# The RWKV of the context between the products of three feed-forwards, in a two-block network on one core

## The chip, the core and the metric

One core of a Trainium2 chip runs the whole network in one launch. The metric is the device time of that launch in microseconds. The kernel before takes 2272.97 us (median of 3 runs, 2269.67 to 2284.12). The engines are PE (TensorE: matmuls; its weight loads are listed apart as PEld), DVE (VectorE), ACT (ScalarE), POOL (GpSimd) and SP (SyncE, which issues the DMAs). Each runs its own instructions in order.

## The reference

256 latent tokens of 1024 features pass through a first block and then, with 256 context tokens, through a second block. All is float32.

```python
def first_block(x, ...):
    for l in range(2):
        x = x + 0.5 * swiglu_ffn(rmsnorm(x, norm_ffn1[l]), ffn1_w_up[l], ffn1_w_down[l])
        x = x + hybrid_mixer(rmsnorm(x, norm_mix[l]), ...)      # pooling and an LRU
        x = x + 0.5 * swiglu_ffn(rmsnorm(x, norm_ffn2[l]), ffn2_w_up[l], ffn2_w_down[l])
    return rmsnorm(x, final_norm)

def second_block(x, c, ctx, c_ctx, ada_w, ada_b, norm_g, ...):
    xc = ctx
    for i in range(2):
        shift, scale, gate = split(silu(c) @ ada_w[i] + ada_b[i], 3)            # and the like of c_ctx
        h  = rms_norm(x,  norm_g[i]) * (1 + scale)   + shift
        hc = rms_norm(xc, norm_g[i]) * (1 + scale_c) + shift_c
        y, yc = rwkv7_mixer(h, hc, ...) if i == 0 else diff_mixer(h, hc, ...)   # attention
        x = x + gate * y;  xc = xc + gate_c * yc

def rwkv7_mixer(h, hc, ...):
    lat, con = rwkv7_streams(h, ...), rwkv7_streams(hc, ...)
    oc_f, sc_f = scan_direction(con, 0, zeros, False);  oc_b, sc_b = scan_direction(con, 1, zeros, True)
    ol_f, _    = scan_direction(lat, 0, sc_f, False);   ol_b, _    = scan_direction(lat, 1, sc_b, True)
    return readout(ol_f + ol_b, lat, ...), readout(oc_f + oc_b, con, ...)
```

The context's RWKV depends on `ctx` and on the modulation alone, and not on the first block. The latents' scans start from the states in which the context's scans end.

## The kernel before, in words

**Large products.** Every large product is made of float32r parts: an operand is split in a high and a low part, and three matmuls (high by high, high by low, low by high) make one step of 128 rows. A class `Weights` streams the weight chunks in the order of use through a ring: a DMA on SP's queue into a raw tile, then per 128x512 piece an ACT copy (`whi`) and a DVE subtraction (`wlo`; `vhi` and `vlo` in the second block). In the mixers a part of these pieces goes to POOL instead (`MIXLO`: numbers such as 4 mean that every fourth low, or high, piece does).

**The order of work** is written out by the program at build time. `Clock` keeps a rough account of the engines' times. Large products are emitted in a fixed order; between them `tick` and `advance` take steps of `Chain`s, which are generators of dependent instructions. A step is emitted once the account says that its inputs are there. A chain that is not `urgent` also waits until DVE and ACT are at most `BACKLOG` (600 ns) ahead of PE. `take` and `until` let the account's time go on (PE then stands idle) until a tile is free or a condition holds.

**Stages.** (1) The first block, latents alone: for each of two layers a feed-forward `f1`, the mixer, a feed-forward `f2`. A feed-forward has 44 upward column tiles (24 matmuls each) and 8 downward ones (66 each): 1584 matmuls of 128x256. A mixer has 1560. (2) `ada` (L1094) computes the modulation meanwhile: of each of 48 column tiles of `ada_w`, in two halves, POOL multiplies 128x512 weights with the two broadcast conditions, 128x1024 elements an instruction, and ACT sums the rows. It goes on only while `calm` is set, which is so in feed-forwards. (3) `enter_ctx` and `enter` (L1253, L1267) form the operands of RWKV; the first four products (`EARLY`) are done with the context's half while the last norm of the latents is computed. (4) `rwkv` (L1354): both sequences lie side by side in tiles of 512 tokens. For each of 8 tiles of 128 channels (j, called a head here) there are four products of 8 steps (k, r, v, gate), the lora products, and then chains: `prepare` (decays, keys, alpha and beta, one set of 9 work tiles `w`), `products` for each sequence (u = 0, 1: pairs of steps within a chunk, into `GE`), `inverse` (for both sequences at once: 32 problems by DVE transposes, 15 steps of two instructions on POOL, and small matmuls), `recur` for each direction (4 chunks of the context, then 4 of the latents, one after the other; each chunk has three groups of small matmuls with DVE or ACT between them), and `readout`. (5) `rwkv_out` (the output product of both sequences, with the first keys and values of the attention) and `attention`.

Most instructions are recorded with the one line L89, that of the helper that counts them, so groups are told apart by the names of their tiles: `ops` and `b` are operands of large products, `q` alpha and beta, `S` the state, `uv`, `rs`, `ro` tiles of the recurrence, `invX`, `invN`, `invt` those of the inverse, `X` also a part of `GE`.

Of the kernel before, what the change touches and what calls it, by code (L numbers as in the profile page):

```python
# [26 lines left out]
class Clock:  # L27
    """A rough account of when the engines get through what was emitted, to order the emission by."""
# [21 lines left out]
    def pressing(self):  # L50
        """Whether this tick can still get full, but only with nothing but large products in it."""
# [11 lines left out]
    def product(self, least, columns, rows):  # L63
        """A product; the array's clock is full in a tick after one with enough columns in it."""
# [8 lines left out]
class Engine:  # L73
    """An engine whose instructions are put on the clock's account."""
# [26 lines left out]
    def product(self, name, out, weights, moving):  # L101
# [3 lines left out]
        elif moving.dtype == F32R:  # L105
            self.clock.product(107, n + 5, rows)
        elif out.shape[0] > 64:
# [20 lines left out]
class Core:  # L128
    """The core's engines, with an account of their time."""
# [9 lines left out]
class Part(tuple):  # L139
    """The two parts of an operand, and when they are there."""  # L140
# [9 lines left out]
class Weights:  # L150
    """Streams weight chunks in the order of use and splits each into two float32r parts."""
# [26 lines left out]
    def queue(self, need=0):  # L178
        while self.queued < min(max(need, 0), len(self.plan)) or (
# [16 lines left out]
            hi = self.pool.tile([128, self.chunk], F32R, tag=self.tag + "hi", bufs=self.nsplit, name=self.tag + "hi")  # L196
            lo = self.pool.tile([128, self.chunk], F32R, tag=self.tag + "lo", bufs=self.nsplit, name=self.tag + "lo")
# [29 lines left out]
    def begin(self):  # L227
        """Splits what has been asked for, before anything else follows."""
# [17 lines left out]
    def tick(self, n):  # L246
        """Goes on with the splitting as far as the engines have time for it."""
# [10 lines left out]
    def get(self, key, keep=0):  # L258
        """The parts of the next chunk; the last `keep` chunks before it are still in use."""
# [18 lines left out]
class Lazy:  # L278
    """Operand pairs that exist once their chains have got there."""
# [12 lines left out]
class Joined:  # L292
    """Chunks that follow one another along the contraction, as one."""
# [8 lines left out]
class Row:  # L302
    """Sums of squares over the features, and what follows from them, for n tokens."""
# [7 lines left out]
AT_ONCE = "at once"  # L311


class Chain:
    """Dependent steps, and when the next of them can start; a step that yields AT_ONCE leaves
    the next one as ready as it was itself."""

    def __init__(self, gen, ready, urgent, rank):
        self.gen, self.ready, self.urgent, self.rank, self.end = gen, ready, urgent, rank, 0.0

# [4 lines left out]
class Base:  # L325
# [15 lines left out]
    def chain(self, gen, urgent=True, start=0.0, rank=0):  # L341
        """Takes up a chain, whose first step waits for `start`; those of a lower rank go first."""
        c = Chain(gen, max(self.clock.end, self.clock.t["PE"], start), urgent, rank)
        if start > self.clock.t["PE"]:
            self.enlist(c)
        else:
            self.step(c)
# [5 lines left out]
    def step(self, c):  # L353
# [11 lines left out]
        if go != AT_ONCE and moved:  # L365
            c.ready = c.end
# [25 lines left out]
    def between(self):  # L392
        """The chains get their turn between two products."""
# [15 lines left out]
    def arrive(self, t):  # L409
        """Lets the time until t go to the chains."""  # L410
# [1933 lines left out]
```

## Time and profile before

| | us |
|---|---|
| median of 3 runs | 2272.97 |
| lowest, highest | 2269.67, 2284.12 |
| span of the profiled execution | 2274.9 |
| PE, PEld busy | 2106.3, 1882.8 |
| DVE, ACT, POOL busy | 1717.8, 1287.4, 861.8 |

The span is that of one profiled execution. Busy time is the time in which an engine has an instruction in it; matmuls are pipelined, so PE counts as busy also where it could take more. The granted clock is the share of TensorE's 2.4 GHz, at 1.0 or 0.5 in any moment. Shares over the whole span hide that the stages have different limits, so the rows below are taken by stage. Stage limits are found by counting large matmuls in program order.

### The profile page before, as it was taken

To read this page: it belongs to the slowest core of one execution; us is meant where nothing else is said; L and a number is where in the kernel's file an instruction comes from. 1 tells how busy PE (TensorE), PEld (TensorE's weight loads), DVE (VectorE), ACT (ScalarE), POOL (GpSimd) and SP (SyncE) were. 2 spreads that over 40 slices of the span, in tenths; PEclk is the share of its full clock that TensorE was granted. 3 is DMA by queue.
4 is the path that set the end of the run, shared out by engine and by line. 5 is a ranking of instruction groups with operands and counts; after the bars stand their busy time and mean duration, and the time that the engine had idled before them with its cause. 6 is when DMAs were issued, how large, how long until landed. Compare 5 with 4: busy or idle time off the path is not lost. (4 is left out here: it accounts for less than half of the span.)

```text
span 2274.9 us, 47231 instructions
## 1 busy us (share of the span) xinstructions
PE 2106.3 (93%) x18172; PEld 1882.8 (83%) x18172; DVE 1717.8 (76%) x3076; ACT 1287.4 (57%) x2970; POOL 861.8 (38%) x1063
## 2 busy tenths in 40 slices
PE   8998998998889889989999988999999998999998
PEld 7988988998889889989999967677677667777878
DVE  6689898888878888897666675765766764558896
ACT  6666684666666666765556543354454342347565
POOL 1154565344544453562001153443543542312331
PEclk9999999999999999999999996899889877869999
DMA  7666554666666565456566310101100110215542
GB/s 243 207 190 202 159 167 131 213 204 200 195 211 209 189 199 193 149 156 197 187 187 183 121 57 24 34 25 39 38 28 30 32 40 9 59 52 165 148 121 89
DMA packets 114098, 300.41 MB, mean 132 GB/s; under 512 B 12624, under 2 KB 18512, under 8 KB 113744
## 3 DMA queue, kind: packets, MB, share of 16 engines
q1 hardware_dynamic: 113872, 297.39, 41.5%
q8 instruction: 142, 2.33, 0.4%
q14 instruction: 84, 0.69, 0.1%
HBM read 292.89 MB, written 4.46 MB: 131 GB/s over the span
## 5 line engine op out<-in xcount | busy, mean ns | idle before, releaser
L89 PE MATMUL ps<-ops,whi 128*128 128x256 f32 x4852 | 895.7, 282 | 19.9 <-ACT ops L89 9.2
L89 DVE TENSOR_TENSOR wlo<-wraw,whi 128x512 fp32r<-128x512 f32 (+2 forms) x792 | 675.4, 890 | 152.0 <-ACT whi L89 147.1
L89 PEld LDWEIGHTS ps<-ops,whi 128*128 128x128 f32 x4852 | 759.2, 190 | 23.9 <-ACT ops L89 9.4
L89 PE MATMUL ps<-ops,wlo 128*128 128x256 f32 x2504 | 710.2, 284 | 28.0 <-DVE wlo L89 28.0
L89 ACT ACTIVATE whi<-wraw 128x512 fp32r<-128x512 f32 (+2 forms) x798 | 437.4, 597 | 130.2 <-issue 60.2
L89 PEld LDWEIGHTS ps<-ops,wlo 128*128 128x128 f32 x2504 | 477.0, 191 | 35.4 <-DVE wlo L89 35.1
L89 PE MATMUL ps<-b,whi 128*128 128x256 f32 x1580 | 322.7, 290 | 31.8 <-ACT b L89 16.8
L89 POOL TENSOR_TENSOR ada<-adaw,ada 128x1024 f32<-128x1024 f32 x96 | 238.7, 2486 | 267.1 <-ACT ada L89 187.9
L89 PEld LDWEIGHTS ps<-b,whi 128*128 128x128 f32 x1580 | 262.2, 197 | 36.3 <-ACT b L89 17.4
L89 PE MATMUL ps<-ops,vhi 128*128 128x512 f32 (+1 forms) x624 | 228.9, 437 | 0.7 <-DVE ops L89 0.7
L89 PE MATMUL ps<-b,wlo 128*128 128x256 f32 x712 | 206.6, 290 | 9.7 <-DVE wlo L89 6.1
L89 DVE TENSOR_TENSOR vlo<-vraw,vhi 128x512 fp32r<-128x512 f32 x202 | 147.0, 740 | 26.3 <-ACT vhi L89 23.0
L89 POOL TENSOR_TENSOR small<-small,mhalf 128x8 f32<-128x8 f32 (+3 forms) x62 | 72.7, 1178 | 243.3 <-DVE small L89 243.1
L89 POOL TENSOR_TENSOR sq<-sq,t 128x256 f32<-128x256 f32 x49 | 45.2, 922 | 279.6 <-ACT t L89 279.1
L89 PEld LDWEIGHTS ps<-b,wlo 128*128 128x128 f32 x712 | 139.8, 196 | 13.5 <-DVE wlo L89 9.4
L89 ACT ACTIVATE ada<-ada 128x512 f32<-128x512 f32 (+1 forms) x193 | 120.6, 627 | 53.2 <-POOL ada L89 53.1
L89 PEld LDWEIGHTS ps<-ops,vhi 128*128 128x128 f32 x624 | 117.2, 201 | 27.2 <-DVE ops L89 1.5
L89 ACT ACTIVATE vhi<-vraw 128x512 fp32r<-128x512 f32 x202 | 121.4, 618 | 28.0 <-PE ps L89 13.7
L89 PE MATMUL ps<-ops,vlo 128*128 128x512 f32 (+1 forms) x312 | 133.5, 428 | 0.2 <-DVE vlo L89 0.2
L89 PE MATMUL ps<-vhi,ops 128*128 128x512 f32 x384 | 126.4, 408 | 2.8 <-ACT ops L89 1.4
L89 ACT ACTIVATE b<-t 128x256 fp32r<-128x256 f32 (+1 forms) x104 | 42.4, 412 | 100.7 <-DVE t L89 100.7
L89 PEld LDWEIGHTS ps<-vhi,ops 128*128 128x128 f32 x384 | 70.2, 190 | 22.1 <-ACT ops L89 3.9
(319 smaller groups left out, 3526.7 us busy)
## 6 DMA issues: line engine op xcount, KB each, us to landing
wraw<-in_ffn_w_up_dram SPq DMA_DIRECT2D x175, 512.0 KB, 3.7
wraw<-in_w_in_dram SPq DMA_DIRECT2D x80, 512.0 KB, 4.0
wraw<-in_ffn_w_down_dram SPq DMA_DIRECT2D x64, 512.0 KB, 3.6
adaw<-in_ada_w_dram SPq DMA_DIRECT2D x96, 256.0 KB, 3.9
vraw<-in_da_in_dram SPq DMA_DIRECT2D x96, 256.0 KB, 2.7
vraw<-in_rw_in_dram SPq DMA_DIRECT2D x60, 256.0 KB, 2.6
wraw<-in_ffn_w_down_dram SPq DMA_DIRECT2D x32, 384.0 KB, 3.6
wraw<-in_w_lru_up_dram SPq DMA_DIRECT2D x32, 320.0 KB, 2.9
```

Source lines behind the costliest of these rows:

```text
L89: return call(*args, **kw)
```

## The change

The context's RWKV is taken out of the RWKV stage and emitted between the products of the feed-forwards `f2` of layer 0, `f1` of layer 1 and `f2` of layer 1. The RWKV stage works on the latents, 256 tokens wide.

- `schedule` puts foreign chunks into the weight stream and their use behind the named products: tiles of the modulation (14 in the first feed-forward, 10 in each mixer, 14 in the last feed-forward), and for each head of the context its four products and its lora. Heads follow one another at 52 us of a feed-forward's time, six in the first two feed-forwards and two in the last. `rw_in` and the lora weights are read and split twice, once for each sequence.
- The modulation is computed by PE: for each of 48 tiles 8 fp32 matmuls of the two conditions (32 columns) with 128 columns of weights, in four column strips, then a copy by ACT and a small matmul that adds the strips.
- `rwkv` is split into `rw_tile` and `rw_lora`, and `prepare`, `products`, `inverse`, `recur` and `readout` take one sequence u with 256 tokens. The context's chains have the lowest rank, are not urgent, may be up to `LATE` (3000 ns) ahead on DVE and ACT, and wait `SLACK_CTX` (400 ns) more before a step of PE. They have one set each of work tiles, of `cq`, `cGE` and of the inverse's tiles, partly in the space that the mixer uses; so the mixer and `enter` wait until no head of the context is open.
- The inverse has 16 problems, held twice to fill 32 columns; the result goes back over a tile in SBUF and an ACT copy.
- The context's last states are stored to DRAM, and the latents' `recur` loads them. Both sequences' z (the gated readout) are stored in halves; the context's are loaded again during the RWKV stage.
- The latents have two sets of work tiles and of the inverse's, four slots of `GE`, four pairs of `q`.
- Upward products of a feed-forward share a PSUM bank in pairs. POOL takes no part of the splitting in the mixers. The early products between the blocks have the latents' half alone.

```diff
-MIXLO = (4, 0), (0, 3), (0, 2), (3, 0)
+MIXLO = (0, 0), (0, 0), (0, 0), (0, 0)
...
-            c.ready = c.end
+            c.ready = c.end + (c.slack if go == ARRAY else 0.0)
...
-                if c.ready <= t["PE"] and (c.urgent or max(t["V"], t["A"]) < t["PE"] + self.BACKLOG):
+                if c.ready <= t["PE"] and (c.urgent or max(t["V"], t["A"]) < t["PE"] + (LATE if c.slack else self.BACKLOG)):
...
-        self.product(W, keys, xs, done)
-        if tag == "f2" and l == 1:
-            self.enter_ctx()
+        self.product(W, keys, xs, done, lambda i: self.other(W, self.extras[tag, l, i]), True)
...
+        self.until(lambda: self.ctx_open == 0)
...
+LATE = 3000
+SLACK_CTX = 400.0
+CTX_AT = [(0, 4 + 52 * n, n) for n in range(6)] + [(1, 4 + 52 * n, 6 + n) for n in range(2)]
...
+                items += [(at + 4 * n, ("rw", b + j)) for n, b in enumerate((8, 0, 16, 24))] + [(at + 16, ("lora", j))]
...
-NQ, NGE, NUV, NSH, NS = 8, 2, 3, 1, 9
+NQ, NGE, NUV, NSH, NS, NINV = 8, 4, 4, 1, 10, 2
...
-            G.tensor_tensor(out=prod, in0=raw, in1=cb[:, :, 512 * h:512 * h + 512], op=ALU.mult)
-            for q in range(2):
-                A.activation(prod[:, q], prod[:, q], AF.Copy, accum_out=sums[:, i, q, h:h + 1])
+        for k in range(KD):
+            g = k % 4
+            self.nc.tensor.matmul(ps[32 * g:32 * g + 32, 0:128], self.cc[:, k, :], w[0][:, k, :],
+                                  start=k < 4, stop=k >= 4, tile_position=(0, 32 * g))
...
+    def go(self, u, gen, rank, urgent=True):
+        if u:
+            self.chain(gen, urgent=urgent, rank=rank)
+        else:
+            self.chain(gen, urgent=False, rank=1000 + rank, slack=SLACK_CTX)
...
+        self.until(lambda: self.now_free(kw, 9 if u else 1))
+        ws = [self.take(kw) for _ in range(9)] if u else self.take(kw)
...
-                self.gemm([(self.half(W, ("rw", i)), 0)], ops, lambda _, ps: self.chain(done(ps)), 512)
+                    self.gemm([(self.half(W, ("rw", i)), 0)], xs, lambda _, ps: done(ps))
...
-            V.transpose(out=N[f, 0:1024].rearrange("p (t s) -> p t s", t=32),
-                        in_=both[f, :, :, f].rearrange("s j p t -> s t j p"))
+            V.transpose(out=N[f, 0:1024].rearrange("p (t o q) -> p t o q", t=32, o=2), in_=twice(ge[f, :, f]))
...
-        G.memset(S, 0.0)
-        for u in range(2):
+        if u:
+            nc.sync.dma_start(out=S, in_=self.states[j][d])
+            yield
+            pp, = yield from self.grab("pp")
+        else:
+            G.memset(S, 0.0)
+            pp, = yield from self.grab("ps")
...
+        if not u:
+            nc.sync.dma_start(out=self.states[j][d], in_=S)
...
+        for j in range(KD):
+            self.chain(self.fetch_z(0, j), urgent=False, rank=100)
```

## Rows read from the trace of the kernel before

**Rows 1.** The page: the span.

```profile
span 2274.9 us, 47231 instructions
```

**Rows 2.** Busy time by stage, feed-forwards and mixers in order, RWKV from 1302.

```profile
core 0: us, PE busy (x) PEld busy (x) DVE busy (x) ACT busy (x) POOL busy (x), PEclk, DMA share, GB/s
0.00:220.20 220.20, 197.88 (x1600) 194.90 (x1601) 168.82 (x290) 136.54 (x308) 71.36 (x119) 0.98 0.65 207
220.20:429.00 208.80, 195.44 (x1570) 191.16 (x1569) 183.94 (x312) 135.54 (x295) 109.62 (x137) 0.97 0.54 170
429.00:647.40 218.40, 196.77 (x1594) 192.31 (x1594) 184.54 (x230) 141.21 (x350) 102.15 (x48) 0.97 0.62 199
647.40:871.50 224.10, 197.59 (x1594) 193.61 (x1593) 191.04 (x241) 144.49 (x356) 101.43 (x47) 0.95 0.64 206
871.50:1078.70 207.20, 192.24 (x1570) 187.84 (x1569) 178.45 (x310) 133.25 (x290) 106.13 (x135) 0.98 0.52 164
1078.70:1267.00 188.30, 187.85 (x1595) 187.44 (x1595) 125.34 (x240) 107.91 (x218) 14.74 (x16) 1.00 0.59 181
1267.00:1302.20 35.20, 35.20 (x258) 33.05 (x257) 24.52 (x54) 19.88 (x39) 3.49 (x10) 1.00 0.35 120
1302.20:2032.00 729.80, 675.97 (x7104) 515.04 (x7103) 469.40 (x994) 317.76 (x775) 293.50 (x501) 0.84 0.12 36
2032.00:2274.90 242.90, 227.35 (x1303) 187.48 (x1303) 191.79 (x411) 150.84 (x344) 59.42 (x52) 0.95 0.43 128
```

**Rows 3.** Stretches again: the downward halves of the first and the last feed-forward.

```profile
139.90:220.20 80.30, 68.69 (x530) 66.60 (x529) 72.34 (x111) 51.77 (x129) 40.66 (x84) 0.94 0.62 192
1203.90:1267.00 63.10, 63.10 (x531) 63.10 (x530) 40.82 (x79) 38.78 (x80) 11.45 (x12) 1.00 0.54 163
```

**Rows 4.** Groups, 429 to 871.5 us: count | busy us, mean ns | idle before <-releaser.

```profile
L89 DVE TENSOR_TENSOR wlo<-wraw,whi 128x512 fp32r<-128x512 f32 x259 | 275.4, 1094 | 50.5 <-ACT whi L89 49.3
...
L89 PE MATMUL ps<-ops,wlo 128*128 128x256 f32 x784 | 223.3, 285 | 21.0 <-DVE wlo L89 21.0
L89 POOL TENSOR_TENSOR ada<-adaw,ada 128x1024 f32<-128x1024 f32 x77 | 190.8, 2478 | 205.3 <-ACT ada L89 163.0 <-DMA adaw<-in_ada_w_dram 21.1 <-ACT t L89 12.6
```

**Rows 5.** Groups again, in the last feed-forward, 1078.7 to 1267 us.

```profile
L89 PE MATMUL ps<-ops,wlo 128*128 128x256 f32 x392 | 109.5, 279 | 0.0
L89 DVE TENSOR_TENSOR wlo<-wraw,whi 128x512 fp32r<-128x512 f32 x130 | 84.9, 691 | 48.1 <-ACT whi L89 48.0
```

**Rows 6.** Groups of PE in the RWKV stage, 1302.2 to 2032 us.

```profile
L89 PE MATMUL ps<-ops,vhi 128*128 128x512 f32 x561 | 211.1, 444 | 0.7 <-DVE ops L89 0.7
L89 PE MATMUL ps<-ops,vlo 128*128 128x512 f32 x281 | 122.3, 435 | 0.2 <-DVE vlo L89 0.2
L89 PE MATMUL ps<-S,q 128*128 128x128 f32 x255 | 62.7, 332 | 7.3 <-DVE S L89 5.8 <-DVE ro L89 0.9 <-ACT ro L89 0.3
...
L89 PE MATMUL ps<-uv,q 128*64 128x64 f32 x448 | 45.2, 264 | 2.1 <-ACT uv L89 1.3 <-DVE uv L89 0.7
```

**Rows 7.** Groups of DVE there: splits; first and last of seven groups of transposes.

```profile
L89 DVE TENSOR_TENSOR vlo<-vraw,vhi 128x512 fp32r<-128x512 f32 x79 | 60.1, 768 | 12.2 <-ACT vhi L89 11.7
...
L89 DVE STREAM_TRANSPOSE GE<-invX 32x1024 f32<-32x1024 f32 x8 | 18.0, 2254 | 5.3 <-PE ps L89 5.2
...
L89 DVE STREAM_TRANSPOSE invX<-GE 32x512 f32<-32x512 f32 x8 | 5.1, 674 | 0.0
...
L89 DVE TENSOR_TENSOR vlo<-vraw,vhi 128x256 fp32r<-128x256 f32 x8 | 3.7, 464 | 0.7 <-ACT vhi L89 0.6
```

**Rows 8.** The stretch of the RWKV stage, instructions on the tile invX alone.

```profile
1302.20:2032.00 729.80, 24.85 (x512) 22.88 (x512) 55.00 (x48) 119.37 (x256) 0.84 0.12 36
```

**Rows 9.** PE in order of time (start us, us): state products of head 0, last lora.

```profile
1402.26 0.63 PE L89 MATMUL ps<-S,q 128*128 128x128 f32 x2
...
1453.59 0.38 PE L89 MATMUL ps<-S,q 128*128 128x128 f32 x2
...
1829.58 0.40 PE L89 MATMUL ps<-lora,vhi 128*128 128x512 f32 x1
```

More of the change, by code (lines that the diff above doesn't have):

```diff
@@ L106, in product @@
             self.clock.product(107, n + 5, rows)
+        elif n <= 2:
+            self.clock.product(111, 4 * n, rows)
         elif out.shape[0] > 64:
@@ L517, in gemm, with product @@
             done(i, pss[i])
-    def product(self, W, keys, xs, done):
+    def product(self, W, keys, xs, done, each=None, pairs=False):
         first = min(3, len(keys))
@@ L524, in product @@
             w = W.get(keys[i])
-            self.gemm([(w, 0)], xs, lambda _, ps: done(i, ps))
+            into = None
+            if pairs and i > 3:
+                if i % 2 == 0:
+                    bank = self.take("ps")
+                into = bank[:, T * (i % 2):T * (i % 2) + T]
+            self.gemm([(w, 0)], xs, lambda _, ps: done(i, ps if into is None else bank), into=into)
+            if each:
+                each(i)
     def rstd_chain(self, row, ps=None):
@@ L1645, in inverse @@
-        self.give(work, kind="inv")
-        run = dict(rec={}, left=2, open=2)
-        self.inverted += 1
+        T1 = X[0:32, 0:512].rearrange("p (q s) -> p q s", q=16)
+        V.transpose(out=T1, in_=ge[0:32, :, 0:32])
+        yield ARRAY
+        Wt = N[32:64, 0:512].rearrange("p (q s) -> p q s", q=16)
+        ps, = yield from self.grab("ps")
+        for p in range(16):
+            mm(ps[32:64, 32 * p:32 * p + 32], ge[0:32, p, 32:64], T1[:, p, :], start=True, stop=True)
+        yield
@@ new lines, in recur @@
+        z["left"] -= 1
+        if z["left"] == 0:
+            self.give(z["GE"], kind=kinds(u, "GE"))
+            self.give(*z["q"], kind=kinds(u, "q"))
+            self.give(z["uv"], kind=kinds(u, "uv"))
+            self.go(u, self.readout(u, j, o_, bv, sg), 10 * j + RANKS[4], URGENT[2])
+        if not u:
+            nc.sync.dma_start(out=self.states[j][d], in_=S)
+            self.clock.end = self.clock.load(1 << 16)
+        self.give(pp, kind="pp" if u and j < KD - 1 else "ps")
+        self.give(state, kind=(kinds(u, "S"), d))
@@ L1767, in readout, with close_z @@
         self.give(y_)
-        run["left"] -= 1
+        yield
+        if u and (j == KD - 1 or self.ops_free):
+            yield from self.close_z(u, j, sg, sg_, ks)
+            return
+        nc.sync.dma_start(out=self.zs[u][j], in_=sg)
+        self.clock.end = self.clock.load(1 << 17)
+        self.give(sg_, kind=ks)
+        if u:
+            self.waiting.append(j)
+        else:
+            self.ctx_open -= 1
+    def close_z(self, u, j, z, tile, kind):
+        tok = slice(T * u, T * u + T)
+        hl = [x[:, j, tok] for x in self.ops]
+        yield from self.hi_lo(*hl, z)
+        self.give(tile, kind=kind)
@@ L1827, in bases @@
             for n in range(KD):
-                while n not in whole or (u and not self.back):
+                while n not in whole:
                     yield
```

862 lines of the change are left out of this document (466 added, 396 removed).

## The prediction

> **What bounds the kernel now.** I read the table of stretches first, then the groups of instructions inside the stretches that differ, then the order of time in one head of the RWKV stage. I cut the stretches where the count of large products in program order says that a feed-forward or a mixer ends (1584 products of 128x256 to a feed-forward, 1560 to a mixer).
>
> Three feed-forwards with the same work take 218.4, 224.1 and 188.3 us [rows 2]. The last one runs at 188.3/1584 = 0.119 us a product with PE never idle: this is the price of a large product when everything it needs is there. The two slow ones are those in which POOL multiplies the modulation's weights (77 instructions of 2478 ns), and there a VectorE split takes 1094 ns on average where it takes 691 ns in the last one; PE waits 21.0 us for splits there and none later [rows 4, 5]. So the first block is bound by PE, with VectorE, held up by POOL, in its way.
>
> The RWKV stage (1302 to 2032 us) is another regime: few loads, 7104 PE instructions of which most are small, PE in use for 676 of 729.8 us, and a granted clock of 0.84 where the feed-forwards have 0.95 to 1.00 [rows 2]. (The clock has two levels, 1.2 and 2.4 GHz; 0.84 is a mean of the two.) VectorE is busy 469 us of it. At the full clock the stretch is worth 729.8 x 0.84 = 613 us. The 842 products of 512 columns and 64 of the lora cost twice the 0.119 us of a 256-column one, 906 x 0.238 = 216 us [rows 6]. If I take PE's own busy time instead of the stretch, 676 x 0.84 = 568. The small products of both sequences thus cost between 568 - 216 = 352 and 613 - 216 = 397 us at the full clock, drains between shapes included: 176 to 198 us a sequence. I began the stretch at the first head's lora; a head comes every (1829.6 - 1302.2)/7 = 75 us, and 202 us pass from the last head's lora to the stage's end [rows 2, 9].
>
> **The change, part by part.**
>
> *The modulation leaves POOL.* The second and third feed-forwards come to the price of the last: 30.1 + 35.8 us [rows 2]. In the first one only the down half is slow, 80.3 us against 63.1 [rows 3]: 17.2. Gain 83 us. Instead PE computes 48 tiles of 8 fp32 products with 32 rows of output in four column strips. The nearest row with 128 moving columns in fp32 takes 246 ns each (62.7/255), the nearest with two strips side by side half that, 101 ns (45.2/448, 64 columns) [rows 6]. One after the other 48 x 8 x 0.246 = 94 us; four at a time 24 us. The pairs of 64 already overlap, so I take 30.
>
> *The context's products.* 34 tiles x 8 x 3 = 816 products x 0.119 = 97 us enter the three feed-forwards. 96 of them stood between the blocks before (35.2 us [rows 2]) to cover the last norm: 11 us go there, but the cover goes too, and the norm's chain of some ten short steps then stands bare; I put back 10.
>
> *The context's small products.* 176 to 198 us; I take the low end, because a step of the context now waits 400 ns longer before its PE instructions are put in line, so PE rarely waits for them: 175. (If the clock fell between them as it does in the old stage, it would be 175/0.84 = 208.)
>
> *VectorE and POOL in the feed-forwards.* A head's inverse is done for 32 columns, whether these hold two sequences or one twice, so its cost is paid again for the context: transposes of 86.7 us in seven groups [rows 7], POOL 119.4 us [rows 8]. The rest halves. VectorE: 469.4 - 63.8 of splits - 86.7 = 319, half 160; with the transposes 86.7 and the second set of splits 63.8 it is 310 us a sequence. Three feed-forwards have 3 x 125.3 = 376 us of their own; 376 + 310 = 686 in 3 x 188.3 + 97 + 175 = 837 us, a share of 0.82. POOL: (293.5 - 119.4)/2 + 119.4 = 206 us in the same 837. What POOL's short instructions do to a split is in the RWKV stage: 768 ns against 691, with POOL busy 0.40 of the time [rows 5, 7]; a quarter of the time gives 50 ns x about 480 splits = 24 us, and VectorE stays below 0.85. No term for it.
>
> The Trainium skill ("SBUF — State Buffer", section Who interferes with whom) says that a VectorE instruction with two SBUF inputs and a POOL instruction that reads SBUF hold each other off for a whole instruction. By that alone the context's POOL work could take up to 206 us from VectorE, whose 892 us would then exceed PE's 837 and cost some 55 us more. The trace so far shows a much smaller toll for short POOL instructions, the 77 ns above.
>
> *The context's turn.* All heads of the context share one set of the tiles that hold alpha, beta and the pairs' products (cq, cGE), from the middle of `prepare` to the end of `recur`. Head 0 of the old stage, almost alone, went from its lora at 1302 over the first state product at 1402.3 to the last at 1453.6 [rows 9]: 51 us for eight steps in the recurrence, so 26 for four, and about 100 before it, of which some 20 come before the tiles are taken. For one sequence the turn lies between 80 (all but POOL's part of the inverse halved) and 130 us (nothing but the recurrence halved, plus the added slack). Six heads have two feed-forwards: 376.6 us and six times (97 + 175)/8 = 34, that is 97 us a head. If a turn is longer, PE waits: for the next head's `rw_lora`, or before the mixer, which now waits until no head is open. At 102 us it is 6 x 5 = 30; I take that. What is queued behind is all of the block, as PE works in order.
>
> *The mixers.* POOL's share of splitting goes to VectorE and ScalarE. Their VectorE is at 178.5 of 207.2 us [rows 2]. Between 0 and 20 us for both; 8.
>
> *The RWKV stage.* PE has 720 products x 0.119 + 8 us of lora + 190 of small ones = 284 us at the full clock. At 0.84 that is 338, or 42 us a head. VectorE's 310 us are 39 a head. The recurrence is 26, and a load of its state. Two sets of work tiles and four slots for the pairs instead of one and two halves let three heads be open, so 43 us a head: 8 us until the first lora, 7 x 43 = 301, and after the last lora its own chain, some 108: 417 us. Bounds: 345 (PE at 0.84 with nothing standing bare) and 490 (55 a head: VectorE at 0.7 of the time, with 2 us for every state that it waits for). Against 729.8 the gain is 313.
>
> *After it.* The context's last tile of z is there long before; its output product, its norm and the first products of its keys can move into the wait for the latents' last head. Before, the context's half of that head came 26 us (four steps of [rows 9]) ahead of the latents' half and its readout after that; so between 0 and 26 us of 242.9 [rows 2]; 15. The stores and loads of 16 states and 16 tiles of z go through SP's queue among few weights (36 GB/s in the old stage [rows 2]) and are hidden by the other open heads; bare they stand in the upper bound.
>
> **The sum,** against the profiled 2274.9 us [rows 1], which is 0.1% over the median of 2272.97: - 83 + 30 + 97 - 11 + 10 + 175 + 30 + 8 - 313 - 15 = - 72, so 2203; less the 2 us to the median, 2200 us. The context costs 97 + 175 + 30 in the first block and frees 313 behind it, so the move itself brings little; most of the gain is POOL's.
>
> **The rivals.** (a) Neither the context's turn nor the last head's chain stands bare: no 30, and a stage of 345: 2203 - 30 - 72 = 2101. For it: the room in the last feed-forward (ScalarE busy 108, VectorE 125 of 188.3 us [rows 2]). Against it: the last head took 202 us from its lora to the stage's end [rows 2, 9]. (b) The latents' stage goes at VectorE's pace, 490 us: 2276, no change. For it: the inverse is not halved, and VectorE's share would rise from 0.64 to 0.75 at 417 us already. (c) Slower: the context's turn takes 130 us on its one set of tiles. PE then waits 6 x 33 = 198 instead of 30 us: 2371. It decides against the change from a turn of 97 + (30 + 72)/6 = 114 us on. For it: in the feed-forwards each step on VectorE or ScalarE stands behind splits, which the code queues up to 2 us ahead of PE (`AHEAD`). Against it: halved instructions, and no second sequence between the steps.
>
> **How the numbers follow.** Forecast 0.45 (2140 to 2255 by itself), (a) 0.22, (b) 0.15, (c) 0.18. About 1% either way, 2250 to 2296, is what a measurement of this kernel can tell from no change. Faster by more: 0.22 and nearly all of 0.45, 0.65; the same: (b) and the edge of the forecast, 0.17; slower: (c), 0.18. The range leaves out the far part of (a) and most of (c): 2095 to 2300 us.
>
> **What would show it.** Right: the first feed-forward's down half near 63 us; splits at 690 ns where no head is open and below 800 where one is; the second and third feed-forward and the last at some 290 us each with a clock above 0.95; the stage of RWKV at 417 us with heads 43 us apart. Wrong: PE idle before the second mixer or before a context's lora by more than 30 us (c); VectorE above 0.85 in the RWKV stage (b); modulation products of 0.25 us one after the other; a clock in the feed-forwards near that of the old stage, which would make the context's small products cost as much as where they were.

## The result, and the profile after

The changed kernel takes 2363.36 us (median; 2353.93 to 2369.86) against 2277.78 us for the kernel before on the same chip: 1.039 times the time, 95% interval 1.034 to 1.044. It is slower, where I forecast 2200 us. The span of the profiled execution is 2362.4 us, against 2274.9 before [rows 1].

The stretches of the changed kernel, cut by the same counts of products as in [rows 2] (first feed-forward in two halves; mixer; the two feed-forwards; mixer; last feed-forward; between the blocks; RWKV stage from the first lora to the last state product; the rest):

```profile
core 0: us, PE busy (x) PEld busy (x) DVE busy (x) ACT busy (x) POOL busy (x), PEclk, DMA share, GB/s
0.00:156.30 156.30, 145.88 (x1322) 140.31 (x1322) 96.73 (x208) 82.05 (x177) 17.42 (x31) 1.00 0.67 222
156.30:219.90 63.60, 63.60 (x535) 63.56 (x531) 47.62 (x109) 36.08 (x71) 6.52 (x70) 1.00 0.69 211
219.90:444.70 224.80, 208.48 (x1750) 200.34 (x1749) 174.75 (x356) 157.16 (x338) 58.13 (x94) 0.96 0.54 171
444.70:799.70 355.00, 336.52 (x3205) 318.99 (x3204) 253.96 (x485) 202.67 (x447) 97.48 (x178) 0.93 0.44 133
799.70:1113.60 313.90, 301.55 (x3008) 282.98 (x3007) 226.43 (x451) 177.77 (x392) 94.56 (x160) 0.97 0.42 130
1113.60:1337.50 223.90, 209.06 (x1750) 201.33 (x1749) 171.79 (x343) 152.13 (x325) 57.54 (x95) 0.95 0.55 174
1337.50:1644.50 307.00, 287.41 (x2855) 271.65 (x2853) 199.20 (x402) 168.29 (x368) 72.48 (x124) 0.95 0.49 156
1644.50:1672.00 27.50, 20.34 (x144) 19.86 (x145) 19.14 (x48) 17.43 (x42) 1.21 (x7) 0.81 0.30 92
1672.00:2124.00 452.00, 391.12 (x4009) 328.66 (x4010) 302.93 (x594) 224.79 (x580) 204.30 (x408) 0.77 0.18 56
2124.00:2362.40 238.40, 222.23 (x1276) 184.66 (x1275) 188.09 (x402) 148.30 (x337) 57.86 (x52) 0.96 0.42 125
```

Read it against [rows 2]. The RWKV stage lost 729.8 - 452.0 = 277.8 us. The three feed-forwards that hold the context came to 355.0 + 313.9 + 307.0 = 975.9 us, where three at the price of the undisturbed one would be 3 x 188.3 = 565: the context and the last 14 tiles of the modulation cost 411 us there. Each mixer is 16 us longer. So the move frees 278 us behind the first block and costs more than that inside it. My forecast had 417 us for the stage and 837 us plus 30 of waiting for the three feed-forwards.

In the first two of these feed-forwards the groups of instructions (count | busy us, mean ns | idle before <-releaser) bear on the waits that I had weighed (`ext` and `cGE` hold the context's inverse):

```profile
L89 DVE TENSOR_TENSOR wlo<-wraw,whi 128x512 fp32r<-128x512 f32 x318 | 227.0, 740 | 45.6 <-ACT whi L89 43.2
...
L89 PE MATMUL ps<-ops,wlo 128*128 128x256 f32 x784 | 223.4, 285 | 0.0
...
L89 PE MATMUL ps<-ext,cGE 16*32 16x16 f32 x384 | 10.9, 198 | 19.8 <-DVE ext L89 19.8
```

A split takes 740 ns, not 1094 [rows 4], and PE no longer waits for one. PE does stand, 19.8 us, in front of products of the context's inverse.

### The profile page after: what moved, and what is told of

Same layout as the page of the kernel before. It is cut to its first block, busy times and chain, and to the rows that moved or that the text cites. A ratio compares the mean times of both kernels' runs of the same rounds, so it can differ in the third digit from the quotient of the medians.

```text
span 2362.4 us, 51110 instructions
## 1 busy us (share of the span) xinstructions
PE 2186.2 (93%) x19836; PEld 2012.3 (85%) x19836; DVE 1680.6 (71%) x3389; ACT 1366.7 (58%) x3075; POOL 667.5 (28%) x1218
## 4 chain that ended last, share of the span: by engine, by line
PE 59%; DVE 15%; POOL 10%; ACT 8%; issue 6%; DMA 2%; SPq 0%; DVEq 0%; ACTq 0%; POOLq 0%
PE ps L89 59%; POOL ext L89 5%; DVE wlo L89 4%; DVE ext L89 2%; ACT whi L89 2%; POOL invt L89 2%; DVE t L89 2%; DVE invN L89 2%; POOL invX L89 2%; ACT L89 1%; DMA wraw<-in_w_in_dram 1%; ACT b L89 1%; DVE b L89 1%; DVE vlo L89 1%; DVE ops L89 1%
## 5 line engine op out<-in xcount | busy, mean ns | idle before, releaser
L89 PE MATMUL ps<-ops,whi 128*128 128x256 f32 x4788 | 938.7, 291 | 18.7 <-ACT ops L89 12.1
L89 DVE TENSOR_TENSOR wlo<-wraw,whi 128x512 fp32r<-128x512 f32 (+2 forms) x912 | 624.5, 717 | 172.8 <-ACT whi L89 167.2
L89 ACT ACTIVATE whi<-wraw 128x512 fp32r<-128x512 f32 (+2 forms) x912 | 510.9, 603 | 225.5 <-PE ps L89 77.2
L89 PE MATMUL ps<-b,whi 128*128 128x256 f32 x1416 | 306.5, 292 | 12.9 <-DVE b L89 12.9
L89 POOL TENSOR_TENSOR small<-small,mhalf 128x4 f32<-128x4 f32 (+3 forms) x70 | 75.3, 1079 | 435.0 <-DVE small L89 430.1
L89 POOL TENSOR_TENSOR ext<-ext 64x78 f32<-64x78 f32 (+5 forms) x280 | 151.4, 542 | 106.6 <-DVE ext L89 87.0
L89 PE MATMUL ps<-ops,vhi 128*128 128x256 f32 (+1 forms) x624 | 157.0, 341 | 4.5 <-ACT ops L89 4.1
L89 PE MATMUL ps<-ext,cGE 16*32 16x16 f32 (+3 forms) x1280 | 80.8, 212 | 27.9 <-DVE ext L89 27.8
L89 PE MATMUL ps<-ops,vlo 128*128 128x256 f32 (+1 forms) x312 | 103.7, 332 | 1.3 <-DVE vlo L89 1.2
L89 ACT ACTIVATE ext<-ps 64x64 f32<-64x64 f32 (+4 forms) x148 | 44.8, 304 | 96.3 <-PE ps L89 51.0
L89 PEld LDWEIGHTS ps<-ext,cGE 16*32 16x32 f32 (+3 forms) x1280 | 64.2, 131 | 39.6 <-DVE ext L89 25.7
```

Of the source, the lines that this page charges most:

```text
L89: return call(*args, **kw)
```

## The experiments

I had three explanations after reading the traces: the modulation on PE was under-priced; the context's small products cost more between large products than in their own stage; the context's turn (rival (c)) makes PE stand. The terms of the sum were then taken one at a time.

**1 and 2: the modulation on PE alone.** The kernel before, with the change's `ada`; in the second one with other places for it:

```diff
+            out["mix", l, t] = [("ada", l, 14 + t)]
+        out["f1", 0, 4 + 3 * i].append(("ada", 0, i))
+        out["f2", 1, 4 + 3 * i].append(("ada", 1, i))
# experiment 2 instead:
+        out["f2", 0, 3 + (3 * i) // 2 + (i // 24)].append(("ada", 0, i))
+        out["f1", 1, 3 + (3 * i) // 2].append(("ada", 1, i))
```

> The kernel before with one part of the change alone: the modulation on PE, its 48 tiles at the change's places (14 in the first feed-forward, 10 in each mixer, 14 in the last), POOL free; the context stays in the RWKV stage and the mixers keep POOL's share of the splits. Theory 1 (the modulation's term was mis-sized): the first down half, the second and third feed-forward come to 63, 188 and 188 us, -83 us together, and the tiles cost what the changed kernel's stretches show, 16 in the first up half, 10 in the last feed-forward and some 12 in each mixer: 50 us, so 2275 - 83 + 50 = 2242 us. Theory 2 (my 30 us was right, and the mixers of the changed kernel lose their 16 us by splitting without POOL): 2275 - 83 + 30 = 2222 us, mixers at 209 to 213 us.

> As the one before it, but with 24 tiles in the second and 24 in the third feed-forward and none elsewhere. Theory 1 (a tile costs by where it stands; among the products of a feed-forward 0.74 us, as the 14 of the last one in the changed kernel): -83 + 48 x 0.74 = 36, so 2228 us, with these two feed-forwards at 206 us each and both mixers at 208. Theory 2 (a tile costs 1.2 us wherever it stands, as the 14 of the first feed-forward in the changed kernel): -83 + 56 = 2248 us.

Measured: 2267.45 us, 0.9965 of the kernel before (0.9925 to 1.0005), and 2272.77 us, 1.0001 (0.9968 to 1.0034). Stretches of experiment 1 (first upward half, first mixer, the two feed-forwards, second mixer, last feed-forward, end), then the two feed-forwards of experiment 2:

```profile
7.00:152.60 145.60, 142.55 (x1322) 136.76 (x1322) 93.97 (x202) 78.33 (x174) 16.62 (x24) 1.00 0.70 232
215.10:441.50 226.40, 205.31 (x1750) 198.16 (x1749) 177.01 (x323) 141.72 (x305) 99.93 (x135) 0.95 0.54 172
441.50:629.90 188.40, 187.83 (x1594) 187.42 (x1593) 125.16 (x231) 100.39 (x200) 8.35 (x10) 1.00 0.62 189
629.90:817.30 187.40, 187.40 (x1595) 187.40 (x1595) 122.69 (x229) 98.21 (x197) 6.03 (x8) 1.00 0.61 186
817.30:1040.50 223.20, 206.00 (x1751) 198.71 (x1750) 178.08 (x320) 141.73 (x305) 102.85 (x137) 0.95 0.54 174
1040.50:1240.00 199.50, 199.14 (x1847) 193.94 (x1846) 126.77 (x255) 107.99 (x230) 15.54 (x16) 1.00 0.63 207
...
1999.90:2263.00 263.10, 236.37 (x1327) 197.86 (x1325) 198.49 (x418) 152.19 (x349) 60.96 (x52) 0.91 0.39 118
```

```profile
408.20:620.00 211.80, 211.63 (x2026) 203.26 (x2025) 128.24 (x256) 103.18 (x223) 7.70 (x10) 1.00 0.71 228
620.00:831.20 211.20, 211.20 (x2026) 203.23 (x2025) 126.08 (x254) 101.73 (x221) 6.01 (x8) 1.00 0.70 224
```

What follows. The gain is as forecast: 218.4 and 224.1 us become 188.4 and 187.4, and the first down half is some 18 us shorter. The price is not: 12.7 us in the first upward half (it ended at 139.9 us [rows 3], now at 152.6), 17.6 and 16.0 in the mixers, 11.2 in the last feed-forward, 57.5 us together for 48 tiles where I had 30. Between the products of a feed-forward a tile costs (211.8 + 211.2 - 376.6)/48 = 0.97 us. The mixers of experiment 1 keep POOL's share of the splits and are as long as those of the changed kernel, so giving that share up costs nothing. And behind all that the end of the kernel, which no part of the edit touches, takes 263 us instead of 242.9; in experiment 2 the RWKV stage takes 754.6 us and the end 264.5. So the sum of neither theory came true (2242 and 2222 us for experiment 1, 2228 and 2248 for experiment 2). Experiments 10 and 11 return to this.

**3: the price of the context's heads.** The changed kernel without them:

```diff
         if not u:
+            product(lambda ps: self.give(ps, kind="ps"))
+            return
...
-            self.ctx_open += 1
-            self.rw_lora(0, i, w)
+            pass
```

> The changed kernel without the context's heads: its 816 large products stay, their results are dropped, and zeros stand for its states and its z; left out are all small products, vector work and lora of the context. It prices this work where the change has put it. Theory 1 (the small work costs far more than the 175 us that were forecast, and nothing else in these feed-forwards is at fault): the three feed-forwards fall from 976 to 188 x 3 + 97 + 10 = 672 us, 304 less, and the kernel to 2058 us. Theory 2 (the forecast's 175 + 30 hold, and the rest is lost by large products that wait for splits or by the modulation): 205 less, 2157 us, with the three feed-forwards at 770 us.

Measured: 2085.41 us, 0.917 (0.910 to 0.924). The sum over its three feed-forwards (the changed kernel's three rows above add up to 975.9 us, with PE busy 925.5 and VectorE 679.6):

```profile
sum 697.90, PE 688.09 PEld 681.83 DVE 422.83 ACT 345.51 POOL 31.68; mean PE 229.36 PEld 227.28 DVE 140.94 ACT 115.17 POOL 10.56
```

The heads cost 975.9 - 697.9 = 278 us, nearer to theory 1 (304) than to my own 205. PE's idle time (span less busy) is 50.4 us with them and 9.8 without: 40.6 us of the 278 are PE standing, 237.4 are PE at work. The granted clock in the three stretches is 1.00, 1.00 and 0.98 without them and 0.93, 0.97 and 0.95 with them. VectorE is at 680 of 976 us; it is not the bound.

**5 and 6: the price of going from large products to small ones.** Into the kernel before, in the up half of its last feed-forward, 512 independent small products, in runs of two and in runs of 32:

```diff
+            if 32 <= self.count < 288 and self.count % 1 == 0:       # 6: % 16
+                for i in range(1):                                   # 6: range(16)
+                    for e in range(2):
+                        h = HALF[e]
+                        mm(self.bank[h, 64 * (i % 8):64 * (i % 8) + 64], self.ident[h, h], self.ident[h, h], start=True, stop=True)
```

> A price list: the kernel before with 512 independent small products (64x64, fp32, the identity with itself, results unused) added to the up half of the last feed-forward, in 256 runs of two, one run after each third large product. Nothing waits for them. Theory 1 (a run has a fixed price): in the changed kernel the way from a large product over a run of one such pair to the next large one is 0.35 us longer than without it, so 256 x 0.35 = 90 us on the 188.3 us of that feed-forward, 278, and 2365 us in all. Theory 2 (only the products count, 0.06 to 0.08 us each): 512 x 0.07 = 36 us, 224 for the feed-forward.

> The same 512 small products in the same stretch, in 16 runs of 32. Theory 1 (a fixed price of a run): 16 x 2.5 us (a run of 64 records in the changed kernel takes 2.5 us) = 40 us, so 228 us for the feed-forward, 50 us less than with runs of two. Theory 2: the same as with runs of two, within 5 us.

Measured: 2379.52 us, 1.044 (1.036 to 1.052), and 2326.41 us, 1.022 (1.013 to 1.031). That up half without small products, with runs of two, with runs of 32 (one fence for each kernel):

```profile
1078.70:1203.90 125.20, 124.75 (x1067) 124.34 (x1067) 84.51 (x162) 69.12 (x138) 3.29 (x4) 1.00 0.61 190
```

```profile
1074.80:1317.30 242.50, 242.50 (x2089) 190.87 (x2089) 82.51 (x161) 68.35 (x135) 2.56 (x4) 1.00 0.30 98
```

```profile
1073.20:1233.90 160.70, 160.70 (x2090) 157.33 (x2089) 83.52 (x161) 68.17 (x135) 2.72 (x4) 1.00 0.47 148
```

A run of two adds (242.5 - 125.2)/256 = 0.458 us, a run of 32 adds (160.7 - 125.2)/16 = 2.22 us. So a product more in a run costs (2.22 - 0.458)/30 = 0.059 us, and the run itself 0.458 - 2 x 0.059 = 0.34 us before the first product is paid for. PE counts as busy throughout, at a clock of 1.00: no wait, no idle time and no lower clock of PE shows this price. PEld, busy for 191 of the 242.5 us, hints at it, and the order of time shows it (runs of two; start us, us):

```profile
1150.41 0.33 PE L89 MATMUL ps<-ident 64*64 64x64 f32 x4
1150.67 0.51 PE L89 MATMUL ps<-ops,whi 128*128 128x256 f32 x2
1151.02 0.28 PE L89 MATMUL ps<-ops,wlo 128*128 128x256 f32 x1
1151.23 0.33 PE L89 MATMUL ps<-ident 64*64 64x64 f32 x4
```

From run to run it is 0.82 us, where the three large products alone take 0.36. Theory 1 holds, and the price is higher than I had read off the changed kernel (0.35 us for a run of one pair), because the first large product behind the run is also late. (A product in fp32 leaves two records, hence x4 for two.)

The Trainium skill ("TensorEngine Tiling (Array Packing)", section Key Properties) says that changing the tiling mode drains TensorE. It gives no time for it. These runs agree that each change over and back is paid for, with 0.34 us, but they don't tell how much of it is that drain: the products change from float32r to fp32 at the same places. In experiment 2 the fp32 product that adds the strips of a tile fills the whole array, and in the order of time it still costs 0.22 us between large products, its own time and that of the late large product behind it included.

**4, 7 and 12: the context's turn.** Three changes of when a step of the context gets its turn:

```diff
-SLACK_CTX = 400.0
+SLACK_CTX = 1500.0        # 4;  7: 0.0
# 12 instead:
+                if c.slack and self.count % 4 and not self.open:
+                    continue
```

`count` goes up by one with each step of three large products; `open` holds once the planner, at a place where it lets its time go on, has gone 40 of its turns without an instruction.

> The changed kernel with one number other: a step of the context waits 1500 ns instead of 400 before its products are put in PE's line. Theory 1 (short runs: what the context's small products cost is paid at each change from large to small products and back, whether their operands are there or not): the three feed-forwards stay within 15 us of 976, since the number of runs stays. Theory 2 (late operands: PE stands at the small products because VectorE and POOL are behind the account): the waits of 1.4 to 3.5 us in front of products of the inverse go, some 20 to 40 us in the three feed-forwards. Theory 3 (the context's turn): a head takes some 30 steps x 1.1 us longer, 140 instead of 106 us, and PE waits for the next head or before the second mixer, 20 to 60 us more.

> The changed kernel with the wait before a context step's products at 0 instead of 400 ns. 1500 ns cost 68 us in the three feed-forwards. Theory 1 (the context's turn already bounds them at 400 ns, as rival (c) has it): the turn gets some 30 steps x 0.4 = 12 us shorter and the three feed-forwards lose about 25 us of their 976, 2338 us in all. Theory 2 (at 400 ns the turn is hidden, and the cost is that of the small products themselves): no gain, within 8 us, or some 10 to 20 us more where PE now stands in front of late operands.

> The changed kernel, in which the context's steps get their turn after each twelfth large product instead of each third: 190 runs of small products instead of 238 among the large ones of the three feed-forwards. At the price of a run from the runs of two and of 32 products, 0.34 us, that is 16 us less for the way between large and small products. Theory 1 (what PE pays for changing decides): the three feed-forwards come to some 960 us. Theory 2 (the context's turn decides: a head's 30 steps wait 0.7 us longer on average, 21 us, and 25 us more in the turn cost 68 us): some 1015 us, with more of PE's standing in front of small products than the 42 us of now.

Measured: 2443.62 us (1.073; 1.066 to 1.080), 2422.94 us (1.062; 1.055 to 1.070) and 2470.67 us (1.083; 1.077 to 1.089). The sums over the three feed-forwards, in this order, one fence for each kernel:

```profile
sum 1044.80, PE 948.87 PEld 892.07 DVE 679.78 ACT 547.22 POOL 261.93; mean PE 316.29 PEld 297.36 DVE 226.59 ACT 182.41 POOL 87.31
```

```profile
sum 1019.40, PE 926.36 PEld 874.42 DVE 681.35 ACT 539.33 POOL 252.97; mean PE 308.79 PEld 291.47 DVE 227.12 ACT 179.78 POOL 84.32
```

```profile
sum 1074.40, PE 936.40 PEld 882.88 DVE 676.95 ACT 552.12 POOL 249.67; mean PE 312.13 PEld 294.29 DVE 225.65 ACT 184.04 POOL 83.22
```

PE stands 95.9, 93.0 and 138.0 us in them, against 50.4 in the changed kernel. From its lora to its last state product head 0 takes 107 us in the changed kernel and 132 us at 1500 ns (in this order):

```profile
489.85 0.28 PE L89 MATMUL ps<-clora,whi 128*128 128x256 f32 x1
...
596.01 0.39 PE L89 MATMUL ps<-cS,cq 128*128 128x128 f32 x2
```

```profile
485.42 0.28 PE L89 MATMUL ps<-clora,whi 128*128 128x256 f32 x1
...
616.64 0.38 PE L89 MATMUL ps<-cS,cq 128*128 128x128 f32 x2
```

In experiment 4 theory 3 is right, beyond its 20 to 60 us (69 in the three stretches). In experiment 7 theory 1 is wrong in sign, and theory 2 in size: 43 us more, not 10 to 20; head 0 takes 118 us there, and why it takes longer with no added wait is not shown. In experiment 12 the turn decides as well (theory 2), and costs 98 us where I expected 39. The trace has 199 runs in place of 248 there, and from start to start the ways between large and small products, waits taken out, come to 63 us instead of 77; that gain of 14 us, expected at 16, is lost six times over to the waits, 87.6 us more.

Where PE stands tells the cause. A head's lora waits until the head before it gives back its work tiles, at the end of its inverse, and while it waits the planner puts no large product in line: the inverse, whose steps on POOL and VectorE follow one another with little for PE between, stands bare. From experiment 12, the last large product before such a stretch, the longest wait in it, and the lora that ends it:

```profile
1528.09 0.28 PE L89 MATMUL ps<-ops,wlo 128*128 128x256 f32 x1
...
1546.94 0.28 PE L89 MATMUL ps<-ext,cGE 16*32 16x16 f32 x2 [17.22 <-DVE ext L89]
...
1563.97 0.58 PE L89 MATMUL ps<-clora,whi 128*128 128x256 f32 x1
```

Stretches of more than 3 us without a large product stand before six of the eight loras in experiments 4 and 12 and before five in experiment 7, and PE's idle time in them is 73, 112 and 69 us of the 95.9, 138.0 and 93.0. In the changed kernel they stand before three loras, 37 us in all, with PE idle for 15. The two longest there (us, PE busy, PEclk, DMA share, GB/s; PE alone):

```profile
764.90:777.80 12.90, 7.58 (x142) 0.61 0.26 83
1448.70:1467.60 18.90, 10.32 (x226) 0.63 0.35 113
```

So what these three experiments add is in the main rival (c)'s wait, and the changed kernel has a little of it.

**8 and 9: the last head's inverse.** The 30 POOL instructions of the latents' last inverse go to VectorE; in 9 the planner still books them on POOL, so that the order of every engine is that of the changed kernel:

```diff
-            E = V if k in STEPS else G
+            E = V if k in STEPS or (u and j == KD - 1) else G
# 9:
+        self.quiet = Engine(nc.vector, "G", self.clock)
+            E = V if k in STEPS else self.nc.quiet if u and j == KD - 1 else G
```

> The changed kernel with the 30 short POOL instructions of the inverse of the latents' last head on VectorE; all else as it was. The 156 us from the last head's first product of the lora to the stage's end were forecast at 108. Theory 1 (POOL's inverses, one head's behind another's, stand bare there: the chain that ended last passes through them from 1967 to 2056 us): the tail loses 10 to 20 us, 2345 to 2352 us in all. Theory 2 (PE's own order and the half clock make the tail): within 4 us of 156.

> The changed kernel with the inverse of the latents' last head on VectorE again, but with its 30 instructions still put on POOL's account in the planner, so that every engine's order of instructions is that of the changed kernel. The same edit without this shortened the tail of the RWKV stage from 156 to 136 us and lengthened what follows from 238 to 269 us. Theory 1 (that loss is the planner's other order behind the edit): the tail near 136 us, the end at 238, 2342 us in all. Theory 2 (VectorE's 30 instructions or the earlier start cost the end its 30 us): the end stays near 265 us and the whole at 2365.

Measured: 2372.83 us (1.041; 1.032 to 1.050) and 2357.61 us (1.033; 1.028 to 1.039). From the last lora to the last state product and from there to the end, in 8 and in 9 (the changed kernel has 156.3 and 238.4):

```profile
1963.20:2099.50 136.30, 124.03 (x1294) 94.80 (x1293) 85.89 (x199) 62.14 (x166) 42.46 (x81) 0.79 0.13 37
2099.50:2368.20 268.70, 237.10 (x1344) 197.07 (x1342) 205.28 (x436) 153.76 (x349) 60.28 (x52) 0.94 0.39 120
```

```profile
1964.80:2118.30 153.50, 136.18 (x1361) 106.14 (x1360) 101.66 (x232) 66.67 (x178) 42.54 (x81) 0.80 0.15 48
2118.30:2356.60 238.30, 221.02 (x1276) 183.36 (x1275) 189.06 (x402) 148.22 (x337) 57.88 (x52) 0.97 0.41 125
```

By experiment 8 alone I would have called POOL's inverse the cause of the tail. Experiment 9 takes that back: in the same order the tail is 153.5 us, 3 less, and the end is 238.3. Its theory 1 is right for the end and wrong for the tail. The 20 us of experiment 8 came from the planner, which dealt the products otherwise (67 fewer PE instructions in the tail than in 9, 68 more behind it), and the end paid 30 us for it. The tail is not the last inverse on POOL; what sets it stays open between PE's queue and the clock (below).

**10 and 11: the modulation again, with the order behind it held.** Experiments 2 and 1, with the planner's account set to that of the kernel before where the second block begins, and without the new price of small products:

```diff
                 K.enter(W)
+                K.rebase()      # t[engine] = that of the kernel before + a whole number of TICK
...
-        elif n <= 2:
-            self.clock.product(111, 4 * n, rows)
```

> The kernel before with the modulation on PE in the second and third feed-forward, and with the planner's account set, where the second block begins, to what it holds there in the kernel before (and the small products' new price taken out of it), so that from there on each engine's order is that of the kernel before. Without this the first block was 42 us shorter and the rest 47 longer. Theory 1 (the rest was lost to the planner's other order): 1261 us up to the first lora, the RWKV stage and the end at 730 and 243 us, 2275 - 42 = 2233 us. Theory 2 (the second block is slower for another reason, such as the modulation's other layout or the clock): 2270 us again, with the RWKV stage at 750 and the end at 260.

> The same for the modulation at the change's own places (14 tiles in the first feed-forward, 10 in each mixer, 14 in the last). Theory 1: 1276 us up to the first lora and the second block as before, 2275 - 27 = 2248 us; so this part of the change is worth 27 us where I forecast 53 (83 - 30). Theory 2: 2265 us again.

Measured: 2234.4 us, 0.980 (0.972 to 0.987), and 2268.08 us, 0.995 (0.991 to 0.999). First block, RWKV stage and end of 10, then of 11:

```profile
0.00:1260.20 1260.20, 1224.78 (x10633) 1196.57 (x10633) 905.53 (x1721) 716.08 (x1516) 268.76 (x415) 0.99 0.61 192
1260.20:2007.50 747.30, 694.45 (x7104) 530.27 (x7102) 469.46 (x994) 317.94 (x775) 293.43 (x501) 0.81 0.11 35
2007.50:2250.40 242.90, 225.08 (x1303) 184.58 (x1302) 191.91 (x411) 150.28 (x344) 59.41 (x52) 0.97 0.42 128
```

```profile
0.00:1278.10 1278.10, 1228.76 (x10632) 1201.07 (x10633) 893.87 (x1722) 719.40 (x1516) 255.13 (x416) 0.98 0.59 189
1278.10:2024.10 746.00, 692.82 (x7104) 528.65 (x7102) 467.05 (x994) 318.17 (x775) 293.91 (x501) 0.81 0.11 35
2024.10:2266.90 242.80, 227.44 (x1303) 187.45 (x1302) 191.64 (x411) 150.81 (x344) 59.35 (x52) 0.95 0.42 128
```

The end is 242.9 and 242.8 us, as before: its 20 us were the planner's order (theory 1). The RWKV stage is not back at 729.8: with the same instructions in the same order it has 747 and 746 us and a granted clock of 0.81 instead of 0.84 [rows 2]. These are single executions, and one program spreads as far: the four of experiment 10 lie between 2223 and 2252 us, with the profiled one the slowest, and the kernel before took 2259 us at a mean clock of 0.937 in one execution and 2292 us at 0.919 in another. So theory 1 is right for the end. For experiment 10 as a whole its 2233 us meets the median of 2234, but the profiled execution misses it by 17 us, so that agreement is in part luck; experiment 11 missed by 20 us, 16 of which are in its RWKV stage. Why the clock differs is open. Experiment 10 is some 2% faster than the kernel before, by four executions: the modulation's part of the change, put into the second and third feed-forward, without the context's move.

## Why the prediction was wrong, by its own steps

The terms of the sum, forecast and measured against the profiled 2274.9 us:

| term | forecast | measured | from |
|---|---|---|---|
| modulation off POOL | -83 | -85 | experiment 1 |
| modulation on PE | +30 | +57 | experiment 1 |
| mixers' splits without POOL | +8 | 0 | experiment 1 against the changed kernel |
| context's large products, norm chain, between the blocks | +97 - 11 + 10 = +96 | +114 | experiment 3: 697.9 - 565 - 11 of modulation = 122, and 27.5 - 35.2 |
| context's heads in the feed-forwards | +175 + 30 = +205 | +278 | experiment 3 |
| RWKV stage | -313 | -278 | stretches |
| the end | -15 | -4 | stretches |
| sum | -72 | +82 | 2357, of 2362.4 |

The heads have 73 of the 154 us between the two sums, the RWKV stage 35, the modulation on PE 27, the context's large products 18 and the end 11, less 10 for the mixers and POOL. The 18 and the 11 are not taken apart.

**The step that failed most is "the context's small products: 175", with "PE rarely waits for them".** I divided the old stage's small products by two sequences and the clock, 176 to 198 us, and took the low end. That carries over a price per product. What I left out is that small products also pay for every run of them. In the old stage those of two sequences stood in 213 runs between large products, 107 for a sequence; in the context's feed-forwards there are 248 runs (counted in the order of time), 35 of which are there without the heads too (experiment 3), so the heads have 213. At 0.34 us a run, an estimate from experiments 5 and 6 for runs of this kind, 106 more runs are 36 of the 62 us by which PE's work of 237 us exceeds the 175. Another 8 are the 64 products of the context's loras (64 x 0.119 us), which stood in no term of the sum. The other 18 are the low end I took and a clock of 0.93 to 0.97; the runs don't part these.

The old stage's runs cost the same between products of 512 columns, by medians in the order of time. There the first small product starts 0.327 us after the last large one, the first large one 0.149 us after the last small one, and the second large one 0.338 us after the first, where large products otherwise start 0.234 us apart. In the changed kernel it is 0.209, 0.148 and 0.222 us, and 0.120. Beyond the large products' own time that is 0.35 us a run in the old stage and 0.34 in the new place.

**The term for the context's turn had its mechanism, at half its size; a like wait stood where I had none.** I had 30 us of PE waiting for the next head's lora or before the mixer. PE stands 40.6 us for the heads: 15 before loras, and 26 among the large products, most of it in front of the inverse's. The 26 are where "PE rarely waits for them" failed. Rival (c) gave 2371 us and the kernel came to 2363, but that is luck: head 0 takes 107 us from its lora to its last state product, so its turn is not 130, and PE stands 15 us before loras, not 198. What (c) had right is that there is no slack in the turn: 25 us more in it cost 69 us (experiment 4). From 400 ns both ways lead up.

**"Four at a time, so I take 30"** was right in its mechanism. The eight products of a tile, in four column strips, are busy 30.9/48 = 0.64 us in experiment 2, not 8 x 0.246:

```profile
L89 PE MATMUL ps<-wraw,ccs 128*32 128x128 f32 x768 | 30.9, 279 | 0.0
```

What I had left out is again the way over and back. A tile costs 0.97 us among large products, as it makes two runs: 0.77 us for its eight products and the late large product behind them, 0.22 for the product that adds the strips (order of time). The 10 tiles of a mixer cost 1.6 each, some of it PE's waiting for ACT's copy of the strips.

**The RWKV stage:** heads come (1967.7 - 1672.0)/7 = 42.2 us apart on average, where I had 43. The last lora comes 296 us after the first, where I had 7 x 43 = 301 (the 8 us that I set before the first lora lie outside the stretch), and then 156 us follow instead of 108. The last lora and the first state products of the last three heads:

```profile
1967.73 0.28 PE L89 MATMUL ps<-lora,vhi 128*128 128x256 f32 x1
...
1995.81 0.39 PE L89 MATMUL ps<-S,q 128*128 128x128 f32 x2
...
2049.31 0.38 PE L89 MATMUL ps<-S,q 128*128 128x128 f32 x2
...
2092.93 0.38 PE L89 MATMUL ps<-S,q 128*128 128x128 f32 x2
```

When the last lora comes, two heads before it have not begun their recurrence. I let three heads be open to get 43 us a head and then charged the tail as that of one head alone; the two don't go together. The clock of 0.77, where I took 0.84, would by itself be worth 391 x (1 - 0.77/0.84) = 33 us of PE's work. The runs don't separate these two, so the cause of the tail's 48 us stays open. VectorE at 303 of 452 us rules out rival (b).

**What held:** the first down half at 63.6 us, splits at 740 ns where heads are open (below 800 forecast, 691 + 50 in the working), the gain from POOL. By the rule of the Trainium skill ("SBUF — State Buffer", section Who interferes with whom) that I weighed, the context's POOL work could have taken 206 us from VectorE and cost some 55 us. The trace does not bear out such a toll: 49 ns on each of 318 splits, 16 us, and VectorE busy for 680 us in the three feed-forwards, where I had 686 without any toll.

**What I said would show a miss** showed it in part: the three feed-forwards are not at 290 but at 355, 314 and 307 us, the clock is below 0.95 in the first. PE idle before a lora, my sign for (c), is there with 15 us, below the 30 that I had set. No row of before shows the price of a run as idle time, but its order of time has it, as told above.

## What to carry to other kernels

When small matmuls move in among large ones, add to the price of the products a second one for each time PE changes over and back (here 0.34 us); PE reads as fully busy while it pays. Where a planner with an account of time orders the program, hold its order behind the edit when a part is measured alone: otherwise a gain of 20 or 40 us upstream comes back as a loss in stretches that the edit does not touch, and gets the wrong name. Where the next piece of a guest's chain waits for the tiles of the last, see what stands in line behind it: here a longer and a shorter wait before the chain's steps both cost (69 and 43 us), because all large products stood behind a lora that waited.

## What the runs showed of the hardware

- Two 64x64 fp32 products between 128x256 products cost 0.458 us, 0.34 of them for the change over and back, with PE busy throughout at a granted clock of 1.00 (experiments 5 and 6). One fp32 product of the whole array with 2 columns costs 0.22 us there (experiment 2).
- The same instructions in the same order took 730, 747 and 746 us in the RWKV stage of three programs, at granted clocks of 0.84, 0.81 and 0.81 (the kernel before, experiments 10 and 11), and executions of one program differ as much (2259 us at 0.937, 2292 at 0.919). The cause is open.
- The granted clock was 1.00 and 1.00 in the two feed-forwards without heads and 0.93 and 0.97 with them (PE idle 1.3 and 30.8 us); where PE stood before a lora, busy 7.6 of 12.9 and 10.3 of 18.9 us, it was 0.61 and 0.63. With 512 small products among large ones and PE never idle it stayed at 1.00 (experiment 5).
